# Moving the mixers' stores to GpSimd, with new mask arithmetic, selection groups and planner costs, in a one-core transformer layer

## The chip, the cores and the metric

The kernel runs on one core of one Trainium2 chip. The metric is the time of one execution on the device in microseconds (us), as the median of several runs. The engines are named as in the profile: PE is TensorE (PEld its weight loads), DVE is VectorE, ACT is ScalarE, POOL is GpSimd, SP is SyncE. ACTq and POOLq mark what the sequencer of an engine does beside its arithmetic, such as issuing a DMA from ACT.

## The reference

One decoder layer over 1024 tokens of width 1024: a half-step SwiGLU, two token mixers side by side, and a second half-step SwiGLU.

```python
x = x + 0.5 * swiglu(rms_norm(x), w1_gate, w1_up, w1_down)
c_q, k_a, v_a, k_idx, w_idx, q_b, k_b, v_b, gate_a, gate_b = split(rms_norm(x) @ w_in)
...
score = sum_h relu(q_idx[h] @ k_idx.T) * w_idx[h]      # indexer, 8 heads of 64
idx = top_k(where(causal, score, -inf), 256)           # 256 keys per query
y_a = softmax(q_a @ k_a[idx].T) @ v_a[idx] @ w_uv      # 8 heads, shared keys and values
...
z = q_b @ k_b.T / 8                                    # stick-breaking, 8 heads of 64
a = exp(log_sigmoid(z) + reverse_cumsum(log_sigmoid(-z)) - log_sigmoid(-z))   # strictly causal
y_b = a @ v_b
...
x = x + (sigmoid(gate_a) * (y_a @ w_oA) + sigmoid(gate_b) * (y_b @ w_oB)) @ w_out
x = x + 0.5 * swiglu(rms_norm(x), w2_gate, w2_up, w2_down)
```

## The kernel before

**Stages.** A SwiGLU stands at each end (0 to about 707 us, and from about 1530 us to the end). Between them lie the mixers: projections of keys, queries and index queries, the indexer's scores, the choice of 256 keys per query, stick-breaking attention, sparse attention, and the output projections. The 1024 queries are cut into 8 blocks of 128; block `i` sees `i + 1` blocks of keys, so its tiles are `128 x (i+1)*128`. Float32 operands are kept as a high and a low part, so that most results leave PSUM twice: ACT copies the high part, DVE subtracts it and keeps the low part. Both are stored to DRAM where a later stage loads them.

**The order.** In the mixers a build-time planner, `Weave`, writes the instruction order of PE, DVE, ACT and POOL. Each piece of work is a generator that yields the engine it wants next and the tiles it waits for; `Weave.cost` gives each instruction a duration, and `Weave.flush` adds up when engines and tiles come free; the ready piece that could start first is written next. The order is then fixed: each engine works through its own list, and an instruction whose input is late holds up everything behind it on that engine. The two SwiGLUs are not planned by `Weave`.

**Names.** `fillers` computes the projections of values, queries, keys and gates (`psf`, weights `wqk...`, `wg...`); `qk_out` evicts queries and keys into `evh` and `evl`, `gate_out` evicts gates into `evg`. These tiles, and `yh`, share one ring of three buffers, `evr`; a buffer is free again when its store has landed. `y_out` evicts a half of a head of stick-breaking attention: `yl` (a ring of one buffer) takes the sum, `yh` its high part, and then `yl` the low part; they are stored to `ybhd` and `ybld`, loaded later as `ybh` and `ybl`. `ka_out` and `key_out` evict values and keys of the sparse mixer.

`topk` finds the threshold of each query bit by bit: 31 rounds, each with one Sign activation on ACT for each block of the group (`junka`), then two small DVE operations. The six blocks with more than 256 keys are split into two groups; each group is one such stream. When the bits are known, one mask for each block is made (lines 1173 to 1186) and stored to `bd`, from where `hidden_keys` loads it as `bias`. Masks of the second group wait for the mark `top0`, and a bias tile for `top0` or `top1` of its group. Sparse attention takes the blocks in the order 1, 0, 5, 4, 7, 6, 3, 2; blocks 1 and 0 need no selection.

In the sticks, PE makes `psz`; ACT takes two sigmoids of it (`left`, `sa`); DVE scans and multiplies; PE transposes (`pstT`), ACT and DVE evict the two parts (`pt`), and PE multiplies by the values (`psy`). In sparse attention PE makes `psL`, DVE adds the bias and takes the maximum (`e`, `mx`, line 1732), ACT exponentiates (line 1744, after a table load at line 1742), DVE normalises (line 1747), PE transposes (`pspT`), and `pt` goes into `pso`. `psob` and `psoa` are output projections.

```python
put_high, put_low = nc.scalar.dma_start, nc.gpsimd.dma_start
```

## Time and profile before

| | us |
|---|---|
| median of 3 runs (2303.51 to 2309.24) | 2306.31 |
| the profiled execution's own time | 2300.48 |
| its span from the first instruction to the last | 2298.7 |

| engine | busy us | share of the span |
|---|---|---|
| PE | 2188.0 | 95% |
| DVE | 1590.1 | 69% |
| ACT | 1111.9 | 48% |
| POOL | 883.6 | 38% |

The shares are means over stages with different limits. For one stage the busy time of each engine in that stretch is compared with the stretch's length; where no engine fills it, the waits say which engine held up which. The profile gives the granted clock of TensorE as a share of full speed (2.4 GHz); 0.5 is its lower level, 1.2 GHz.

### The profile page before, as it was taken

The page shows a single profiled execution, that of the slowest core. Times are in us where ns is not written, and L with a number is a line of the kernel's source. Part 1 is how long each engine was busy: PE and PEld are TensorE (multiplying, and loading weights), DVE is VectorE, ACT ScalarE, POOL GpSimd, SP SyncE. Part 2 cuts the span into 40 slices and gives each one's busy share as a digit, 9 for nine tenths or more (in the row PEclk, how much of TensorE's full clock was granted, in tenths as well). Part 3 has the DMA queues.
Part 4 walks back from the last instruction along what each step waited for, and adds up shares of the span by engine and source line. Part 5 has one row for each costly group of instructions (what it writes and reads, how often), then busy time and mean ns, then how long its engine had stood idle before and what let it go on. Part 6 is the DMA issues. An engine that isn't in the chain of part 4 may idle for free.

```text
span 2298.7 us, 30186 instructions
## 1 busy us (share of the span) xinstructions
PE 2188.0 (95%) x10460; PEld 1808.7 (79%) x10460; DVE 1590.1 (69%) x2512; ACT 1111.9 (48%) x2133; POOL 883.6 (38%) x648
## 2 busy tenths in 40 slices
PE   7999999999999898889999699999999999999999
PEld 6788888888889777667788578877878888888877
DVE  5765656678862897667698877862476565667675
ACT  4323232344452479989988456633342323233443
POOL 3555555432262444211122133146345555543233
PEclk9999999999999999999999799999999999999999
DMA  5233333587663243645464533357323333358755
GB/s 166 75 117 97 114 95 114 167 310 239 165 215 113 81 133 101 172 97 120 112 142 115 173 112 96 127 182 253 118 65 106 101 108 99 110 167 288 244 161 183
DMA packets 252537, 330.64 MB, mean 144 GB/s; under 512 B 20576, under 2 KB 155376, under 8 KB 252384
## 3 DMA queue, kind: packets, MB, share of 16 engines
q1 hardware_dynamic: 235264, 288.83, 42.1%
q0 software_dynamic: 7488, 24.16, 2.8%
q10 hardware_dynamic: 9632, 15.73, 2.0%
q8 instruction: 82, 1.34, 0.2%
q14 instruction: 71, 0.58, 0.1%
HBM read 234.78 MB, written 93.88 MB: 143 GB/s over the span
## 4 chain that ended last, share of the span: by engine, by line
PE 67%; DVE 12%; ACT 10%; DMA 5%; issue 5%; POOL 1%; ACTq 1%; SPq 0%; DVEq 0%; POOLq 0%
PE p L676 5%; PE p L677 5%; PE p L675 4%; ACT junka L1130 4%; PE pc L466 3%; PE pc L467 3%; PE pc L468 3%; PE pd L468 3%; PE pd L466 3%; PE pd L467 3%; PE pa L468 3%; PE pa L466 3%; PE pa L467 3%; PE pb L468 2%; PE pb L467 2%
## 5 line engine op out<-in xcount | busy, mean ns | idle before, releaser
L1130 ACT ACTIVATE junka<-u,cand,sig 128x1024 bf16<-128x1024 f32 (+5 forms) x186 | 182.7, 982 | 22.6 <-DVE cand L1127 10.9
L1566 DVE TENSOR_TENSOR_SCAN left<-left 128x640 f32<-128x640 f32 (+3 forms) x64 | 92.8, 1450 | 3.8 <-ACT left L1558 3.8
L1615 DVE TENSOR_TENSOR pt<-pstT,pt 128x512 fp32r<-128x512 f32 (+1 forms) x96 | 51.2, 551 | 21.0 <-ACT pt L1613 20.4
L1732 DVE CUSTOM_DVE_ANT_0 e<-psL,bias 128x512 f32<-128x512 f32 (+3 forms) x96 | 49.4, 550 | 14.4 <-PE psL L1769 14.4
L1615 DVE TENSOR_TENSOR pt<-pspT,pt 128x512 fp32r<-128x512 f32 x72 | 46.6, 684 | 18.0 <-ACT pt L1613 18.0
L1744 ACT ACTIVATE e<-e,nm 128x256 f32<-128x256 f32 (+7 forms) x64 | 49.4, 774 | 18.5 <-DVE nm L1739 17.3
L1667 PE MATMUL pstT<-ident,sa 128*128 128x128 f32 x288 | 46.7, 276 | 12.1 <-DVE pt L1615 10.3
L1823 PE MATMUL pspT<-ident,e 128*128 128x128 f32 x288 | 42.1, 286 | 16.0 <-DVE ri L1746 9.0
L1569 DVE TENSOR_TENSOR sa<-sa,left 128x639 f32<-128x639 f32 (+3 forms) x64 | 53.1, 829 | 5.0 <-ACT sa L1560 1.8
L676 PE MATMUL p<-bT,bS 128*128 128x512 f32 x132 | 51.9, 393 | 2.9 <-DVE bT L377 2.9
L1634 POOL DMA_DIRECT2D ybld<-yl x16 | 8.8, 551 | 118.6 <-DVE yl L1632 79.7
L1667 PEld LDWEIGHTS pstT<-ident,sa 128*128 128x128 f32 x288 | 34.4, 140 | 25.1 <-DVE pt L1615 16.8
L1613 ACT ACTIVATE pt<-pspT 128x512 fp32r<-128x512 f32 x72 | 39.5, 596 | 29.6 <-PE pspT L1823 29.3
L1823 PEld LDWEIGHTS pspT<-ident,e 128*128 128x128 f32 x288 | 35.3, 146 | 22.4 <-DVE e L1747 9.5
L676 PE MATMUL p<-aT,aS 128*128 128x512 f32 x132 | 51.6, 391 | 1.0 <-DVE aT L377 1.0
L1479 DVE SCALAR_TENSOR_TENSOR u<-relu,WI,u 128x512 f32<-128x512 f32 (+1 forms) x70 | 49.6, 727 | 4.2 <-ACT relu L1472 3.0
L677 PE MATMUL p<-bT,bS 128*128 128x512 f32 x132 | 51.5, 393 | 1.0 <-POOL bS L377 1.0
L1613 ACT ACTIVATE pt<-pstT 128x512 fp32r<-128x512 f32 (+1 forms) x96 | 46.6, 501 | 9.8 <-PE pstT L1667 7.7
L677 PE MATMUL p<-aT,aS 128*128 128x512 f32 x132 | 50.5, 390 | 0.0
L1560 ACT ACTIVATE sa<-psz 128x512 f32<-128x512 f32 (+2 forms) x96 | 47.0, 503 | 5.0 <-ACT evg L1063 2.4
L1558 ACT ACTIVATE left<-psz 128x512 f32<-128x512 f32 (+2 forms) x96 | 45.3, 496 | 7.8 <-DVE cand L1161 1.6
L1472 ACT ACTIVATE relu<-psdot 128x512 f32<-128x512 f32 (+1 forms) x80 | 39.9, 520 | 16.6 <-DVE u L1479 9.9
(3061 smaller groups left out, 8296.4 us busy)
## 6 DMA issues: line engine op xcount, KB each, us to landing
aw<-in_w_down_dram SPq DMA_DIRECT2D x33, 512.0 KB, 4.8
bw<-in_w_down_dram SPq DMA_DIRECT2D x33, 512.0 KB, 4.5
a0r<-in_w_gate_dram SPq DMA_DIRECT2D x22, 512.0 KB, 4.3
a1r<-in_w_up_dram SPq DMA_DIRECT2D x22, 512.0 KB, 4.9
b0r<-in_w_gate_dram SPq DMA_DIRECT2D x22, 512.0 KB, 4.1
b1r<-in_w_up_dram SPq DMA_DIRECT2D x22, 512.0 KB, 4.8
x<-in_x_dram SPq DMA_DIRECT2D x16, 512.0 KB, 6.3
gd<-evg ACTq DMA_DIRECT2D x32, 256.0 KB, 2.8
```

What stands on the lines that cost most here:

```text
L466: nc.tensor.matmul(ps, a[:, c], b[k][:, HI], start=start and k == 0, stop=False, skip_group_check=True)
L467: nc.tensor.matmul(ps, a[:, c], b[k][:, LO], start=False, stop=False, skip_group_check=True)
L468: nc.tensor.matmul(ps, a[:, l], b[k][:, HI], start=False, stop=k == 3, skip_group_check=True)
L675: nc.tensor.matmul(ps[q][m], S[:, h], T[:, HI], start=p == 0, stop=False)
L676: nc.tensor.matmul(ps[q][m], S[:, h], T[:, LO], start=False, stop=False)
L677: nc.tensor.matmul(ps[q][m], S[:, l], T[:, HI], start=False, stop=p == last)
L1130: nc.scalar.activation(junks[1][:, 0:(i + 1) * P], score[i], AF.Sign, scale=sig[:, b:b + 1], bias=cand.bitcast(F32)[:, b:b + 1], accum_out ...
L1566: nc.vector.tensor_tensor_scan(back, back, back, 1.0, op0=ALU.mult, op1=ALU.bypass)
L1613: nc.scalar.activation(pt[:, off:512], tp[:, off:512], AF.Copy)
L1615: nc.vector.tensor_sub(pt[:, 512 + off:1024], tp[:, off:512], f32(pt[:, off:512]))
L1667: nc.tensor.transpose(tp[:, q * P:(q + 1) * P], A[n + q][:, j * P:(j + 1) * P], ident)
L1823: nc.tensor.transpose(tp[:, q * P:(q + 1) * P], E[n + q][:, j * P:(j + 1) * P], ident)
```

## The change

**Stores.** 74 stores that ACT issued (queries and keys, gates, the high parts of `va`, `ka` and `yh`) are issued by POOL (`put_low`), each as a step of its own that the planner places. **Costs.** The planner's ACT instructions with an accumulator cost 0.09 more and are ready 0.05 sooner, a store on ACT would cost 0.37 where it cost 0.05, and some DVE forms cost 0.06 or 0.11 more. **Groups.** The groups of the selection are blocks (5, 4, 2) and (6, 7, 3), which were (7, 2, 3) and (4, 5, 6). **Masks.** A mask is made from one Sign activation on ACT with the threshold as bias and the count as its accumulator, one comparison of its 16-bit result, the scan, a subtraction and one comparison. Before, there were two comparisons with the float32 scores, the scan, a comparison with a product, a sum and a scaling, all on DVE.

```diff
@@ Weave.cost and Weave.flush @@
-            return 0.055 + n / 1190 + 0.22 * (len(outs) > 1), 0.1 + 0.15 * (len(outs) > 1)
+            return 0.055 + n / 1190 + 0.31 * (len(outs) > 1), 0.1 + 0.1 * (len(outs) > 1)
...
-    groups = ((7, 2, 3), (4, 5, 6))
+    groups = ((5, 4, 2), (6, 7, 3))
@@ qk_out @@
             nc.scalar.activation(th, ps, AF.Copy, scale=sc)
-            put_high(qkd[nh_][pr * P:(pr + 1) * P, cols], f32(th))
             yield DVE, ps, th
             nc.vector.scalar_tensor_tensor(tl_, ps, sc, f32(th), op0=ALU.mult, op1=ALU.subtract)
-            give(ps, th)
+            give(ps)
+            yield POOL, th
+            put_low(qkd[nh_][pr * P:(pr + 1) * P, cols], f32(th))
+            give(th)
@@ gate_out @@
             nc.scalar.activation(ev, ps, AF.Sigmoid)
-            put_high(gd[g * P:(g + 1) * P, cols], ev)
-            give(ps, ev)
+            give(ps)
+            yield POOL, ev
+            put_low(gd[g * P:(g + 1) * P, cols], ev)
+            give(ev)
@@ topk @@
-            nc.vector.tensor_mul(Tf, Tf, sig)
+            nc.vector.scalar_tensor_tensor(fix, Tf, -1.0, sig, op0=ALU.mult, op1=ALU.mult)
...
-                yield DVE, (x2, 3)
+                yield ACT, (x2, 3), fix
...
-                nc.vector.tensor_scalar(eq, score[i], Tf[:, c], None, op0=ALU.is_equal)
-                yield DVE
-                nc.vector.tensor_scalar(gt, score[i], Tf[:, c], 0.0, op0=ALU.is_gt, op1=ALU.add, accum_out=cnt[:, c])
-                nc.vector.tensor_scalar(rem[:, c], cnt[:, c], -1.0, float(TOPK), op0=ALU.mult, op1=ALU.add)
+                nc.scalar.activation(gt, score[i], AF.Sign, bias=fix[:, c], accum_out=cnt[:, c])
+                yield DVE, gt
+                nc.vector.tensor_scalar(eq, gt, 0.0, STEP, op0=ALU.is_equal, op1=ALU.mult)
+                nc.vector.tensor_scalar(rem[:, c], cnt[:, c], -0.5 * STEP, (TOPK - 0.5 * nk) * STEP, op0=ALU.mult, op1=ALU.add)
                 yield DVE
                 nc.vector.tensor_tensor_scan(cum, eq, eq, 0.0, op0=ALU.add, op1=ALU.bypass)
                 yield DVE
-                nc.vector.scalar_tensor_tensor(eq, cum, rem[:, c], eq, op0=ALU.is_le, op1=ALU.mult)
-                yield DVE
-                nc.vector.tensor_add(gt, gt, eq)
+                nc.vector.scalar_tensor_tensor(rem[:, c], cum[:, nk - 1:nk], 0.5, rem[:, c], op0=ALU.mult, op1=ALU.add)
+                nc.vector.tensor_sub(eq, cum, gt)
...
-                nc.vector.tensor_scalar(bias, gt, -NEG, NEG, op0=ALU.mult, op1=ALU.add)
+                nc.vector.tensor_scalar(bias, eq, rem[:, c], NEG, op0=ALU.is_gt, op1=ALU.mult)
```

The stores in `ka_out`, `key_out` and `y_out` are moved in the same way; that of `yh` now stands on POOL ahead of that of `yl`. Line numbers of the changed kernel are a few higher than before.

What the planner makes of it differs in many places. On POOL, among the gates' weight splits (`wg10l` and so on, a subtraction of two 128x1024 tiles), there stood before:

```order
L974 TENSOR_TENSOR wg10l<-wg10r,wg10h 128x1024
L974 TENSOR_TENSOR wg11l<-wg11r,wg11h 128x1024
L1634 DMA ybld<-yl 64x512
L974 TENSOR_TENSOR wg12l<-wg12r,wg12h 128x1024
L1634 DMA ybld<-yl 64x512
L974 TENSOR_TENSOR wg13l<-wg13r,wg13h 128x1024
```

and now:

```order
L976 TENSOR_TENSOR wg10l<-wg10r,wg10h 128x1024
L1642 DMA ybhd<-yh 64x512
L1070 DMA gd<-evg 128x512
L1647 DMA ybld<-yl 64x512
L1642 DMA ybhd<-yh 64x512
L1070 DMA gd<-evg 128x512
L1647 DMA ybld<-yl 64x512
L976 TENSOR_TENSOR wg11l<-wg11r,wg11h 128x1024
L1070 DMA gd<-evg 128x512 x2
L976 TENSOR_TENSOR wg12l<-wg12r,wg12h 128x1024
```

So stores of gates and of `yh` stand between the splits, and pairs of gate stores behind a split.

On ACT, where the sticks end and the first exponentials (`e`) begin, there stood before:

```order
L1063 ACTIVATE evg<-psf 128x512
L1064 DMA gd<-evg 128x512
L1613 ACTIVATE pt<-pstT 128x256
L1628 ACTIVATE yh<-yl 64x512
L1630 DMA ybhd<-yh 64x512
L1613 ACTIVATE pt<-pstT 128x128
L972 ACTIVATE ob2h<-ob2r 128x1024
L1622 ACTIVATE yl<-psy 64x512
L1063 ACTIVATE evg<-psf 128x512
L1064 DMA gd<-evg 128x512
L1742 ACT_TABLE_LOAD
L1744 ACTIVATE e,ssum<-e,nm 128x256 x2
```

and now:

```order
L1633 ACTIVATE yl<-psy 64x512
L1624 ACTIVATE pt<-pstT 128x384
L1624 ACTIVATE pt<-pstT 128x256
L1639 ACTIVATE yh<-yl 64x512
L1624 ACTIVATE pt<-pstT 128x128
L1755 ACT_TABLE_LOAD
L1757 ACTIVATE e,ssum<-e,nm 128x256 x3
L1633 ACTIVATE yl<-psy 64x512
L1757 ACTIVATE e,ssum<-e,nm 128x256
L1639 ACTIVATE yh<-yl 64x512
L1181 ACTIVATE gt,cnt_6038<-u_7226,fix_11658 128x896
L1757 ACTIVATE e,ssum<-e,nm 128x256 x2
```

The table load moved from behind the last `yl` and the last gate to ahead of that `yl`, directly behind the last `pt` of the sticks, and the masks' Sign (`gt`) of block 6 stands among the exponentials.

On PE, at the same place, the last products `psy` of the sticks stood behind projections of gate 7, of which these are the last:

```order
L307 MATMUL psf<-mhi_5243,wg7h 128x512
L308 MATMUL psf<-mlo_5251,wg7h 128x512
L309 MATMUL psf<-mhi_5243,wg7l 128x512
L307 MATMUL psf<-mhi_5244,wg7h 128x512
L308 MATMUL psf<-mlo_5252,wg7h 128x512
L309 MATMUL psf<-mhi_5244,wg7l 128x512
L1647 MATMUL psy<-pt,vv 128x128
L1649 MATMUL psy<-pt,vv 128x128
L1823 MATMUL pspT<-ident,e 128x128 x8
```

and now there stands, with no projection of a gate left:

```order
L1680 MATMUL pstT<-ident,sa 128x128 x2
L1660 MATMUL psy<-pt,vv 128x512
L1662 MATMUL psy<-pt,vv 128x512
L1660 MATMUL psy<-pt,vv 128x384
L1662 MATMUL psy<-pt,vv 128x384
L1680 MATMUL pstT<-ident,sa 128x128
L1660 MATMUL psy<-pt,vv 128x256
L1662 MATMUL psy<-pt,vv 128x256
L1660 MATMUL psy<-pt,vv 128x128
L1662 MATMUL psy<-pt,vv 128x128
L1836 MATMUL pspT<-ident,e 128x128 x8
```

The gates' projections moved ahead, into the sticks. The order inside the two SwiGLUs is the same on every engine.

## Rows read from the trace of the kernel before

**Rows 1.** The page's first part: busy us, share of the span, instructions.

```profile
PE 2188.0 (95%) x10460; PEld 1808.7 (79%) x10460; DVE 1590.1 (69%) x2512; ACT 1111.9 (48%) x2133; POOL 883.6 (38%) x648
```

**Rows 2.** Stretches of the mixers: length, busy us by engine, clock, DMA share, GB/s.

```profile
707.00:840.00 133.00, 122.16 (x724) 106.33 (x725) 88.48 (x150) 56.93 (x116) 49.87 (x49) 0.96 0.38 106
840.00:1160.00 320.00, 285.31 (x1453) 228.00 (x1452) 229.01 (x431) 290.19 (x608) 75.52 (x67) 0.97 0.49 121
1160.00:1283.00 123.00, 122.52 (x634) 100.48 (x632) 110.14 (x211) 95.36 (x201) 27.07 (x17) 1.00 0.50 140
1283.00:1318.00 35.00, 16.79 (x64) 11.58 (x64) 28.46 (x93) 16.56 (x46) 4.00 (x4) 0.70 0.49 163
1318.00:1530.00 212.00, 202.17 (x1043) 167.75 (x1043) 158.56 (x425) 110.96 (x220) 60.69 (x54) 0.98 0.39 125
```

**Rows 3.** Waits of PE, 840 to 1160 us: total us, times, longest.

```profile
PE pstT L1667 <- DVE pt L1615: 10.3, 10, 2.2
PE psz L1589 <- ACT sa L1560: 10.1, 6, 2.3
PE psqt L1445 <- DVE qx L1441: 4.8, 1, 4.8
```

**Rows 4.** ACT's evictions with stores, 840 to 1160 us: count, busy us, mean ns, idle before.

```profile
L1063 ACT ACTIVATE evg<-psf 128x512 f32<-128x512 f32 x17 | 10.4, 614 | 1.1 <-PE psz L1593 0.6 <-ACT yh L1628 0.5
L1051 ACT ACTIVATE evh<-psf 128x512 fp32r<-128x512 f32 x11 | 6.6, 600 | 0.0
L1628 ACT ACTIVATE yh<-yl 64x512 fp32r<-64x512 f32 x8 | 5.0, 620 | 0.5 <-DVE pt L1615 0.5
```

**Rows 5.** ACT in order of time around one store: start us, length us.

```profile
935.50 0.33 ACTq L1052 DMA_DIRECT2D khd<-evh  x1
935.88 0.81 ACT L1130 ACTIVATE junka<-u,cand,sig 128x512 bf16<-128x512 f32 x1 [0.41 <-ACT evh L1051]
```

**Rows 6.** POOL's stores of `evl`: issue in ns, landing; then landing of ACT's `gd`.

```profile
L1057 POOL DMA_DIRECT2D kld<-evl x8: 539/575/631, 814.7 to 987.3; - x8
DMA to landing us min/median/max: 2.3/6.3/10.6
...
DMA to landing us min/median/max: 2.0/2.8/10.3
```

**Rows 7.** All engines in order of time at the sticks' end: start us, length us.

```profile
1279.09 0.54 POOL L1634 DMA_DIRECT2D ybld<-yl  x1 [9.70 <-DVE yl L1632]
...
1282.73 0.28 PE L1649 MATMUL psy<-pt,vv 128*128 128x128 f32 x1
...
1284.84 0.59 ACT L1622 ACTIVATE yl<-psy 64x512 f32<-64x512 f32 x1 [1.08 <-DMA ybld<-yl]
...
1286.44 1.28 ACT L1742 ACT_TABLE_LOAD   x1 [0.39 <-ACT evg L1063]
...
1290.38 0.49 ACT L1744 ACTIVATE e<-e,nm 128x256 f32<-128x256 f32 x1
...
1292.05 1.30 PE L1823 MATMUL pspT<-ident,e 128*128 128x128 f32 x3 [9.05 <-DVE ri L1746]
```

**Rows 8.** The masks' lines on DVE, 1283 to 1318 us: count, busy us, mean ns.

```profile
L1178 DVE TENSOR_TENSOR_SCAN cum<-eq 128x640 f16<-128x640 f16 (+2 forms) x3 | 5.2, 1748 | 0.0
L1175 DVE TENSOR_SCALAR_CACHE_REDUCE gt<-u,T 128x640 f16<-128x640 f32 (+2 forms) x3 | 3.0, 1000 | 0.0
L1180 DVE SCALAR_TENSOR_TENSOR eq<-cum,rem,eq 128x640 f16<-128x640 f16 (+1 forms) x2 | 1.9, 944 | 0.0
L1173 DVE TENSOR_SCALAR eq<-u,T 128x768 f16<-128x768 f32 (+1 forms) x2 | 1.3, 646 | 0.0
L1182 DVE TENSOR_TENSOR gt<-gt,eq 128x640 f16<-128x640 f16 (+1 forms) x2 | 1.0, 520 | 0.0
L1186 DVE TENSOR_SCALAR cum<-gt 128x640 bf16<-128x640 f16 (+1 forms) x2 | 0.7, 335 | 0.0
```

**Rows 9.** ACT's Sign on 896 keys, 707 to 1320 us: count, busy us, mean ns.

```profile
L1130 ACT ACTIVATE junka<-u,cand,sig 128x896 bf16<-128x896 f32 x31 | 35.6, 1148 | 2.4 <-ACT evg L1063 1.6 <-ACT yh L1628 0.5
```

More of the change, by code (lines that the diff above doesn't have):

```diff
@@ L129, in cost @@
             return 0.17 + n * (0.5 if any(a.dtype in (F32, F32R, I32) for a in wide) else 0.25) / 960, 0.08
-        return 0.07 + n / 960, 0.08
+        slow = getattr(i, "is_scalar_tensor_tensor", False) or len(ins) == 1 and len(outs[0].shape) == 2 and n > outs[0].free_size()
+        return 0.07 + 0.06 * slow + 0.11 * (outs[0].shape[0] < P) + n / 960, 0.08
     def hop(self, name, eng):
@@ L151, in flush @@
                 else:
-                    t = max(t, self.free[eng]) + (0.55 if eng == POOL else 0.05)
+                    t = max(t, self.free[eng]) + (0.55 if eng == POOL else 0.37)
                     self.free[eng], t, eng = t, t + 2.4 + mb / 0.25, "DMA"
@@ L906, in trunk @@
         ctx1.close()
+    STEP = 2.0 ** -12
     WI = cst.tile([P, NT, H], F32, name="WI")
-    groups = ((7, 2, 3), (4, 5, 6))
+    groups = ((5, 4, 2), (6, 7, 3))
     order = groups[0] + groups[1]
@@ L1179, in topk @@
                 yield DVE
-                nc.vector.scalar_tensor_tensor(eq, cum, rem[:, c], eq, op0=ALU.is_le, op1=ALU.mult)
-                yield DVE
-                nc.vector.tensor_add(gt, gt, eq)
-                give(tiles[0], tiles[2])
+                nc.vector.scalar_tensor_tensor(rem[:, c], cum[:, nk - 1:nk], 0.5, rem[:, c], op0=ALU.mult, op1=ALU.add)
+                nc.vector.tensor_sub(eq, cum, gt)
+                give(tiles[2])
                 bias = tiles[1].bitcast(BF16)[:, 0:nk]
                 yield DVE
-                nc.vector.tensor_scalar(bias, gt, -NEG, NEG, op0=ALU.mult, op1=ALU.add)
+                nc.vector.tensor_scalar(bias, eq, rem[:, c], NEG, op0=ALU.is_gt, op1=ALU.mult)
+                give(tiles[0])
                 yield POOL, tiles[1]
@@ L1306, in ka_out @@
             nc.scalar.activation(va[:, 0:P], ps[:, 64:192], AF.Copy)
-            put_high(vad[0][:, m], f32(va[:, 0:P]))
+            yield POOL, va
+            put_low(vad[0][:, m], f32(va[:, 0:P]))
             yield DVE, bank, va
@@ L1319, in key_out @@
             nc.scalar.activation(h_, ps, AF.Copy)
-            put_high(kad[0][:, cols], f32(h_))
+            yield POOL, ka
+            put_low(kad[0][:, cols], f32(h_))
             yield DVE, ps, ka
@@ L1629, in y_out @@
             cols = slice(c * 512, c * 512 + 512)
-            put_high(ybd[0][h * HD:(h + 1) * HD, cols], f32(yh[0:HD]))
+            yield POOL, yh
+            put_low(ybd[0][h * HD:(h + 1) * HD, cols], f32(yh[0:HD]))
             yield DVE, yl, yh
             nc.vector.tensor_tensor(yl[0:HD], yt, f32(yh[0:HD]), op=ALU.subtract)
+            give(yh)
             yield POOL, yl
             put_low(ybd[1][h * HD:(h + 1) * HD, cols], yt)
-            give(yl, yh)
+            give(yl)
         def value_products(h, c, pts, outs):
```

## The prediction

> **What bounds the kernel now.** I read the page's first part first: PE is busy 95% of the span [rows 1], so all that any change of order can give back is PE's idle time, and time in which PE runs at its lower clock. The change touches the mixers alone, so the next view is the table of stretches [rows 2], cut where the character of the work changes. In its rows compare PE's busy time with the length. From 707 to 840 us 10.8 us are missing, from 840 to 1160 us 34.7, from 1160 to 1283 us 0.5, from 1283 to 1318 us 18.2, and from 1318 to 1530 us 9.8. So there are two places to look at: the long stretch in which sticks, selection rounds and projections run together, and the short one in which the sticks end and sparse attention begins.
>
> In the long stretch ACT is busy 290.2 of 320 us [rows 2]. The page doesn't count a store that ACT issues as busy time, but it occupies the engine: behind an `evh` the store goes out at 935.50, and the next activation starts at 935.88, 0.41 us after the eviction ended [rows 5]. ACT evicts 17 gates, 11 query or key tiles and 8 `yh` there [rows 4], and each has a store: 36 x 0.41 = 14.8 us. With them ACT is occupied 305 of 320 us, 95%. The waits of PE agree that ACT is the limit: it waited 10.1 us for `sa` and 10.3 us for `pt` from DVE, which itself follows ACT's `pt` [rows 3]; 20.4 us in all. The stretch from 1160 to 1283 us is PE's own: nothing done to ACT or DVE can shorten it.
>
> At the sticks' end the rows in order of time tell the story [rows 7]. The last product of the sticks ends at 1283.0. The first exponential needs the table load, which starts at 1286.44, because ACT first runs the last `yl` and the last gate; that `yl` waited until 1284.84 for its one buffer, whose store POOL had issued at 1279.09, 5.75 us before. PE starts its first `pspT` at 1292.05, after 9.05 us idle. The granted clock is 0.70 over the stretch [rows 2]: part of it ran at 1.2 GHz after that idleness. DVE is busy 28.5 of the 35 us, and 13.1 of those are the masks of the second group [rows 8], because blocks 5 and 4 come right behind blocks 1 and 0 and belong to that group.
>
> **The change part by part.** *Stores off ACT.* Of the 74 stores, 36 lie in the long stretch and are worth 14.8 us of an engine occupied 95% of it. Not all of it comes back: the wait for `qx`, 4.8 us [rows 3], doesn't hang on ACT. Bounds: nothing, if PE then waits for DVE's half of each eviction instead; 20.4 us, if both waits go, helped by a planner that now knows how long ACT takes and puts projections where PE used to wait. I take 13, near the stores' own price, because the price is a sum of rows and the help by the planner is not. The stores before 840 us lie on an ACT that is busy 57 of 133 us, and those from 1160 to 1283 us beside a full PE [rows 2]: nothing.
>
> *Stores onto POOL.* Each takes 0.55 us to issue, at most 0.63 in this line [rows 6]; 36 x 0.55 = 20 us on a POOL that is busy 75.5 of 320 us [rows 2]. That is hidden by POOL's own idle time. What it delays is the landing, and so the ring of three buffers. Landing took 2.3 to 10.6 us from POOL and 2.0 to 10.3 from ACT [rows 6], so it is much the same; the new part is the queue on POOL, a split or a store ahead. Cover: 36 evictions and 11 further `evl` in 320 us are one buffer each 6.8 us, so three buffers stand 20 us of holding; a hold of 11 us with 3 us of queue fits. I take nothing; the bound above is among the rivals.
>
> On the same POOL stores the Trainium skill speaks against this change (SBUF — State Buffer, section SBUF: two separate sides): a DMA issued from GpSimd has its descriptors written by that engine, and DVE in a two-port mode locks it out meanwhile, so that the store waits although no wire is busy. The trace doesn't show it, since no issue of this line took over 0.63 us with DVE busy 229 of 320 us [rows 2, 6]. By the page's measured pair, 0.62 us alone and 3.1 us beside a DVE copy, 36 stores would hold POOL for 112 us, an estimate from that page; POOL has 244 us free, so the sum stays the same.
>
> *Groups and masks at the sticks' end.* Blocks 5 and 4 are now in the first group, whose masks are made during the sticks, so bias tiles are there when `psL` of block 5 comes. The masks of blocks 6 and 7 still fall among the exponentials of blocks 1 and 0, but are cheaper on DVE: scans 1.748 x 1920 / 768 = 4.4 us (1920 keys for both, 768 the mean of the three sizes in the row), subtractions 0.520 x 1920 / 704 = 1.4, four 16-bit operations 0.335 x 1920 / 704 / 2 = 0.46 on average, 1.8, and small ones 0.6: 8.2 us where there were 13.1 [rows 8]. In exchange ACT gets two Signs, about 1.15 and 1.3 us [rows 9] and 0.2 each to read the accumulator. DVE is the busier of the two there, so I take 4.9 less half of the 2.9, about 3.5.
>
> *The table load.* It moves ahead of the last `yl`, directly behind the last `pt`, so three exponentials run at once. The fourth still stands behind `yl`, which needs the store of the `yl` before. From the end of `yh` that takes some 0.8 for DVE's low part (an estimate from ACT's 0.62 for the same tile [rows 4] and the steps between engines), 5.75 from the issue to `yl`, and 0.59 [rows 7]: 7.2 us. The end of `yh` is now some 1.2 us ahead of the last product (the last `pt`, its low part and the product, each of 128 columns and near the 0.28 of that product), so the fourth exponential starts 6.0 us behind it, where it was 7.4 (1290.38 less 1283.0). That is 1.4 us; with a landing of 2.3 us it would be 4. I take 2. With less idleness, less of the stretch runs at the lower clock: PE's 16.8 us at 0.70 are 5 us lost; I take 2 of these back. Together 3.5 + 2 + 2 = 7.5 us. Bounds: a loss of 3, if the two Signs delay each group of exponentials in full and the landing takes 10 us; 18 if all idle time goes.
>
> *The drain.* Before, projections of gate 7 stood between the last products; now none does. The last half head has four steps of transposing, ACT's `pt`, DVE's `pt` and a product. A round is at least an eviction by ACT, 0.6 us for 512 columns [rows 4], and as much again on DVE, and some of these rounds are bare. I charge 3 us, between nothing and 6.
>
> *The rest.* The index stage (10.8 us idle) keeps its order but for stores; the sparse part (9.8 us idle) runs the same work with the projections spread anew. I take nothing, give or take 3 us.
>
> Sum: -13 - 7.5 + 3 = -17.5 us against the profiled execution: a span of 2298.7 becomes 2281, its own time 2300.5 becomes 2283. That execution stands 5.8 us below the median of 2306.3, so the median becomes 2289.
>
> **The rivals.** *All of it comes back.* If the new order fits the engines well, the long stretch gives 20.4 us, the lower clock in it (0.97 of 285 us is 8.6 us) goes as well, and the sticks' end gives 10: together 39 us less 3 for the drain, or 2270. For it: the waits are short and many, which is what an order made with wrong durations gives. Against it: PE's order is fixed, so each wait must go by itself. *Nothing comes back.* ACT's freed 14.8 us turn into waits for DVE, whose `pt` already ends 10.3 us of PE's waits, and the drain eats the sticks' end: -5 to 0, or 2303. For it: DVE is busy 229 of 320 us and holds scans of 1.4 us. *POOL holds the ring.* A store waits on POOL behind a step that isn't ready, its buffer is not free, ACT's next eviction stands still, and with it all of ACT. It decides where a buffer is held over 20 us, three times the 6.8 us above, or where three are taken within a few us. If each of the 32 gate evictions waited 0.8 us, that is 26 us on ACT against 14.8 saved, 11 us slower, or 2317. Against it: in that stretch no wait of the 17 gate evictions was put down to a landing, with landings up to 10.3 us in the run [rows 4, 6]. The rule of the Trainium skill (SBUF — State Buffer, section SBUF: two separate sides) would act at this place and in this sense.
>
> **How the numbers follow.** Chances: my forecast (10 to 28 us less) 0.53, all comes back 0.14, nothing comes back 0.20, the ring 0.13. A measurement of this kernel tells about 0.3%, 6.9 us, from no change. The forecast and the first rival are faster than that, and a little of the second; the third is slower: faster 0.67, same 0.20, slower 0.13. The range goes from 2264, somewhat beyond the first rival, to 2311, where it leaves out most of the third. The forecast's own range is 2278 to 2297.
>
> **What would show it.** No store on ACT's queue; in the stretch of about 840 to 1150 us PE's waits for `sa` and `pt` under half of 20.4 us; the sticks' end with the table load within 1 us of the last product and masks of about 8 us; a drain of bare `pt` rounds of about 3 us. Wrong would be: waits of ACT's `evg` or `evh` for landings of over 5 us in sum, POOL issues well over 0.63 us, or PE's missing time in the long stretch still near 35 us with DVE named.

## The result, and the profile after

The changed kernel takes 2275.53 us (median of 4 runs, 2274.65 to 2278.45), the kernel before 2306.49 us in the runs beside it. The ratio is 0.9868, with a 95% interval of 0.9851 to 0.9885: 30 us faster, 26 to 34. Between the two profiled executions it is 2300.48 less 2276.41, 24.1 us. That is in the forecast's sense and inside the predicted range, 13.5 us better than the forecast of 2289.

The first part of the page, to be held against [rows 1]: PE's busy time is about the same, and POOL has 74 instructions more.

```profile
PE 2183.0 (96%) x10460; PEld 1811.1 (80%) x10460; DVE 1576.1 (69%) x2500; ACT 1110.5 (49%) x2145; POOL 925.9 (41%) x722
```

The stretches of the mixers, with columns as in [rows 2], cut at the last product of the sticks (1275.5) and at the first `psob` (1315.2):

```profile
840.00:1160.00 320.00, 296.77 (x1506) 239.32 (x1505) 232.57 (x424) 292.25 (x620) 106.27 (x110) 0.97 0.50 126
1160.00:1275.50 115.50, 110.96 (x572) 90.83 (x570) 100.01 (x199) 99.54 (x209) 33.66 (x35) 0.99 0.51 155
1275.50:1315.20 39.70, 26.61 (x87) 19.14 (x87) 36.09 (x136) 20.70 (x57) 2.99 (x6) 0.64 0.30 88
1315.20:1508.00 192.80, 190.89 (x1024) 161.49 (x1023) 148.45 (x395) 106.85 (x213) 61.09 (x53) 0.99 0.43 137
```

PE's missing time in the long stretch went from 34.7 to 23.2 us. Behind the sticks it was 18.2 + 9.8 = 28.0 us in the last two rows of [rows 2], and is now 13.1 + 1.9 = 15.0. The last product of the sticks ends 7.5 us sooner (1275.5 for 1283.0), the first `psm` starts 22.4 us sooner (1499.1 for 1521.5), and the SwiGLU behind it gives the rest. So what lies ahead of the last product gave a third, and what lies behind it two thirds.

PE's waits from 840 to 1160 us, against [rows 3]:

```profile
PE psf L308 <- DVE evl L1055: 8.1, 2, 7.8
PE pstT L1680 <- DVE sa L1580: 5.6, 4, 2.4
PE psz L1600 <- ACT sa L1571: 3.9, 2, 3.5
...
PE pstT L1680 <- DVE pt L1626: 1.4, 3, 0.6
```

The waits for ACT's `sa` and DVE's `pt` fell from 20.4 to 5.3 us, as said; that for DVE's part of `sa`, which the prediction didn't count, rose from 1.5 to 5.6. New is a wait of 7.8 us, and its cause is the ring of three buffers. In order of time on POOL, DVE and PE:

```profile
941.34 0.60 POOL L1058 DMA_DIRECT2D qhd<-evh  x1 [3.07 <-ACT evh L1053]
...
955.88 0.69 DVE L1055 SCALAR_TENSOR_TENSOR evl<-psf,evh 128x512 fp32r<-128x512 f32 x1 [10.12 <-DMA qhd<-evh]
...
956.63 0.80 PE L308 MATMUL psf<-mhi,wqk10323h 128*128 128x512 f32 x1 [7.76 <-DVE evl L1055]
```

DVE can't write `evl` until the `evh` of the projection before has landed, 14.4 us after its issue at 941.34, and PE's next projection has no bank until `evl` is out.

The sticks' end in order of time, against [rows 7]:

```profile
1274.39 1.28 ACT L1755 ACT_TABLE_LOAD   x1
...
1275.21 0.33 PE L1662 MATMUL psy<-pt,vv 128*128 128x128 f32 x1 [0.35 <-DVE pt L1626]
...
1277.54 0.59 ACT L1633 ACTIVATE yl<-psy 64x512 f32<-64x512 f32 x1 [0.27 <-DMA ybld<-yl]
...
1278.43 0.51 ACT L1757 ACTIVATE e<-e,nm 128x256 f32<-128x256 f32 x1 [0.29 <-DVE nm L1752]
...
1279.59 0.96 PE L1836 MATMUL pspT<-ident,e 128*128 128x128 f32 x2 [4.05 <-DVE nm L1752]
```

The table load starts 1.15 us ahead of the end of the last product, the fourth exponential 2.9 us behind it, and PE is idle 4.05 us there where it was 9.05. Ahead of it PE waits once more: its row at 1268.93 has 3.89 us for DVE's `pt`. In that time DVE ended the selection of the second group, and one of its small operations ran as long as a subtraction on POOL:

```profile
1264.26 2.35 POOL L976 TENSOR_TENSOR ob2l<-ob2r,ob2h 128x1024 fp32r<-128x1024 f32 x1 [9.36 <-ACT ob2h L974]
1264.28 2.35 DVE L1142 TENSOR_SCALAR T<-T 128x3 int32<-128x3 int32 x1
...
1268.93 0.66 PE L1680 MATMUL pstT<-ident,sa 128*128 128x128 f32 x4 [3.89 <-DVE pt L1626]
```

### The profile page after: what moved, and what is told of

Read it like the earlier page. It is cut to its first block, busy times and chain, and to the rows that moved or that the text cites. A ratio compares the mean times of both kernels' runs of the same rounds, so it can differ in the third digit from the quotient of the medians.

```text
span 2274.6 us, 30225 instructions
## 1 busy us (share of the span) xinstructions
PE 2183.0 (96%) x10460; PEld 1811.1 (80%) x10460; DVE 1576.1 (69%) x2500; ACT 1110.5 (49%) x2145; POOL 925.9 (41%) x722
## 4 chain that ended last, share of the span: by engine, by line
PE 70%; DVE 10%; DMA 7%; ACT 6%; issue 5%; POOL 2%; SPq 0%; ACTq 0%; DVEq 0%; POOLq 0%
PE p L677 5%; PE p L678 5%; PE p L676 5%; PE pc L467 3%; PE pc L469 3%; PE pc L468 3%; PE pd L469 3%; PE pd L467 3%; PE pd L468 3%; PE pa L469 3%; PE pa L467 3%; PE pa L468 3%; ACT junka L1136 2%; PE pb L467 2%; PE pb L469 2%
## 5 line engine op out<-in xcount | busy, mean ns | idle before, releaser
L1136 ACT ACTIVATE junka<-u,cand,sig 128x768 bf16<-128x768 f32 (+4 forms) x186 | 183.3, 985 | 10.8 <-DVE cand L1133 9.0
L1577 DVE TENSOR_TENSOR_SCAN left<-left 128x640 f32<-128x640 f32 (+3 forms) x64 | 88.1, 1378 | 3.4 <-ACT left L1569 3.3
L1580 DVE TENSOR_TENSOR sa<-sa,left 128x639 f32<-128x639 f32 (+3 forms) x64 | 58.6, 918 | 3.7 <-ACT sa L1571 0.4
L1680 PE MATMUL pstT<-ident,sa 128*128 128x128 f32 x288 | 47.0, 278 | 11.1 <-DVE sa L1580 5.6
L1624 ACT ACTIVATE pt<-pspT 128x512 fp32r<-128x512 f32 x72 | 39.7, 596 | 36.2 <-PE pspT L1836 35.9
L1757 ACT ACTIVATE e<-e,nm 128x256 f32<-128x256 f32 (+7 forms) x64 | 49.4, 774 | 13.0 <-DVE nm L1752 11.3
L1680 PEld LDWEIGHTS pstT<-ident,sa 128*128 128x128 f32 x288 | 34.7, 141 | 22.4 <-DVE pt L1626 9.0
L1624 ACT ACTIVATE pt<-pstT 128x512 fp32r<-128x512 f32 (+1 forms) x96 | 46.3, 505 | 11.2 <-PE pstT L1680 10.1
L1899 POOL TENSOR_TENSOR o<-o,gate 128x512 f32<-128x512 f32 x16 | 21.8, 1360 | 65.2 <-ACT o L1894 65.2
```

Source lines behind the costliest of these rows:

```text
L1136: nc.scalar.activation(junks[1][:, 0:(i + 1) * P], score[i], AF.Sign, scale=sig[:, b:b + 1], bias=cand.bitcast(F32)[:, b:b + 1], accum_out ...
L1577: nc.vector.tensor_tensor_scan(back, back, back, 1.0, op0=ALU.mult, op1=ALU.bypass)
L1624: nc.scalar.activation(pt[:, off:512], tp[:, off:512], AF.Copy)
L1680: nc.tensor.transpose(tp[:, q * P:(q + 1) * P], A[n + q][:, j * P:(j + 1) * P], ident)
```

## The experiments

Each run is compared with the kernel before on the same chip; gains in us are its ratio's distance from 1, times 2304.

**One part at a time on the kernel before.** The edits are the four parts of the diff above, each alone.

```diff
@@ stores only: here gate_out; the same in qk_out, ka_out, key_out and y_out @@
-            put_high(gd[g * P:(g + 1) * P, cols], ev)
...
+            yield POOL, ev
+            put_low(gd[g * P:(g + 1) * P, cols], ev)
...
@@ groups only @@
-    groups = ((7, 2, 3), (4, 5, 6))
+    groups = ((5, 4, 2), (6, 7, 3))
@@ masks only: topk as in the change, of which one line @@
+                nc.scalar.activation(gt, score[i], AF.Sign, bias=fix[:, c], accum_out=cnt[:, c])
@@ costs only: Weave.cost and Weave.flush as in the change, of which one line @@
-                    t = max(t, self.free[eng]) + (0.55 if eng == POOL else 0.05)
+                    t = max(t, self.free[eng]) + (0.55 if eng == POOL else 0.37)
```

> The kernel before with only the stores moved: 74 stores issued by GpSimd as steps of their own; planner costs, groups and masks as before. Stores theory: this alone gives about 11 to 15 us, since 36 stores of 0.41 us leave ScalarE in the long stretch; the waits of PE for sa and pt there, 20.4 us before, fall under 10 us, and the sticks' end and the sparse part change by less than 4 us. Costs theory (the stores help only with a planner that knows ScalarE's real durations): under 5 us. Ring theory: waits for landings eat it, 0 or some us slower.

> The kernel before with only the groups (5, 4, 2) and (6, 7, 3). Stores theory: 3 to 6 us faster, all of it behind the sticks, where the masks of blocks 5 and 4 no longer fall among the first exponentials; idle time of PE from the last product of the sticks to the first psm, 27.7 us before, falls by 3 to 6. Groups theory: the fall of 12.9 us in that idle time which the changed kernel shows is all due to the groups, so 10 to 15 us faster. Costs theory: no change, within 3 us.

> The kernel before with only the new masks (one Sign on ScalarE, a 16-bit comparison). Stores theory: 2 to 5 us faster, since the masks between 1283 and 1318 us take DVE some 8 instead of 13 us. Groups theory: 0 to 2 us. Masks theory: 6 us or more faster, DVE being what the sparse part waits for. Against all of them: the Signs delay the exponentials, and it is 1 to 3 us slower.

> The kernel before with only the planner's three cost lines (a store on ScalarE 0.37 instead of 0.05, accumulators 0.31 and 0.1, slower forms of DVE); all stores are still ScalarE's. Stores theory: within 5 us of the kernel before, since ScalarE keeps its 14.8 us of stores in the long stretch. Costs theory: 10 to 20 us faster, with PE's waits for sa and pt between 840 and 1160 us falling from 20.4 to under 10 us without any store moved.

Stores 2287.29 us, 0.9934 (0.9917 to 0.9951); groups 2291.59, 0.9949 (0.9934 to 0.9965); masks 2296.91, 0.9974 (0.9962 to 0.9986); costs 2290.49, 0.9940 (0.9925 to 0.9955). Each alone is a gain, 15.2, 11.8, 6.0 and 13.8 us. They add up to 47, and together they give 30, so they overlap. The times of stores, groups and costs are about those of the theories named after them; that of the masks lies at the bound between two.

The stores' gain is as large as the prediction's first term, but it isn't found where the term put it. PE's missing time from 840 to 1160 us is 35.5 us, where it was 34.7: the waits for `sa` and `pt` fell to 10.1 us, and one wait of 11.9 us, put down to a round of the selection, came in their place.

```profile
840.00:1160.00 320.00, 284.46 (x1461) 230.84 (x1460) 231.83 (x440) 285.82 (x613) 101.86 (x107) 0.96 0.49 123
```

```profile
PE pstT L1675 <- ACT junka L1134: 11.9, 1, 11.9
```

The groups' gain lies behind the first `psob`: from there to the first `psm` PE's missing time is 3.8 us, where it was 9.8.

```profile
1320.40:1509.50 189.10, 185.27 (x1007) 156.89 (x1005) 151.69 (x419) 109.11 (x222) 54.22 (x49) 1.00 0.41 131
```

The run that told most is the last, costs alone. Its long stretch, and PE's waits there (of the two that are in question, both rows stand here):

```profile
840.00:1160.00 320.00, 308.03 (x1592) 251.12 (x1591) 240.62 (x427) 283.75 (x604) 85.26 (x71) 0.98 0.51 130
```

```profile
PE psz L1590 <- ACT sa L1561: 3.1, 3, 2.4
...
PE pstT L1668 <- DVE pt L1616: 0.9, 3, 0.5
```

No store has moved, 41 are ACT's in this stretch, and the waits are 4.0 us; PE works 308.0 of 320 us. ACT is about as full as before: 283.8 us busy and 19.0 idle at the 41 stores make 303 us, against 290.2 and 16.0 at 36 stores, 306. So these waits didn't need a much freer ACT: another order removes them too. What it won there it lost behind the sticks. The rows are PE's waits from 1266 to 1345 us:

```profile
PE psL L1769 <- DVE mx L1733: 12.7, 3, 11.2
PE pspT L1824 <- DVE e L1748: 9.2, 6, 3.0
PE psya L308 <- ACT o L1882: 8.1, 1, 8.1
```

**The queue alone, in an unchanged order.** The planner is told an engine for each store that differs from the engine that issues it, so that the order of all arithmetic stays word for word the same.

```diff
+            eng = self.plan.get(n, str(i.engine).split(".")[-1])
@@ kernel before, its order, the 74 stores on GpSimd @@
+    put_high, put_low = put_as(nc.gpsimd.dma_start, ACT), nc.gpsimd.dma_start
@@ changed kernel, its order, the 74 stores on ScalarE @@
+    put_back, put_low = put_as(nc.scalar.dma_start, POOL), nc.gpsimd.dma_start
```

> The kernel before in its own order, in which only the queue of the 74 stores changes: the planner still counts them as ScalarE's, so TensorE, VectorE and the arithmetic of ScalarE and GpSimd keep their order. Occupancy theory (each store takes 0.41 us of a ScalarE that is the limit in the long stretch): 10 to 15 us faster, PE's waits for sa and pt between 840 and 1150 us fall from 20.0 to under 10 us. Order theory (PE waits there because its list was written with wrong durations, and ScalarE has time enough): within 4 us of before, those waits stay above 14 us, and the gain of the run with only the stores moved was the new order. Ring theory: slower, with waits of ScalarE for landings.

> The changed kernel in its own order, in which only the queue of the 74 stores goes back to ScalarE: the planner still counts them as GpSimd's, and all arithmetic keeps its order. Occupancy theory: 8 to 15 us slower than the changed kernel (2284 to 2291 us), with PE's waits for sa and pt in the long stretch back above 15 us. Order theory: within 4 us of the changed kernel's 2275.5; less idle time at 956 us, where a landing held PE for 7.8 us, may even make it 3 faster.

The order of before with stores on POOL: 2296.92 us, 0.9972 (0.9959 to 0.9985), 6.5 us faster (3.5 to 9.4), between the two theories. Its waits:

```profile
PE psz L1599 <- ACT sa L1570: 5.7, 5, 2.3
PE pstT L1677 <- DVE pt L1625: 5.6, 5, 2.6
...
PE psf L308 <- ACT evg L1073: 4.3, 2, 3.0
```

The two waits fell from 20.4 to 11.3 us, and a new one for `evg` took 4.3 of that. So the 6.5 us are net of that wait, in an order that was not made for stores on POOL.

The order of after with stores on ACT: 2273.77 us, 0.9880 (0.9860 to 0.9900), not to be told from the changed kernel's 0.9868. Its long stretch:

```profile
840.00:1160.00 320.00, 300.83 (x1527) 242.81 (x1526) 234.17 (x430) 297.26 (x629) 84.18 (x72) 0.98 0.51 128
```

ACT is busy 297.3 us and issues 41 stores, and PE still does 300.8 us of work, more than in the changed kernel. But these stores don't cost ACT 0.41 us each. To be held against [rows 5]:

```profile
937.07 0.57 ACT L1063 ACTIVATE evh<-psf 128x512 fp32r<-128x512 f32 x1
937.55 0.80 ACT L1146 ACTIVATE junka<-u,cand,sig 128x512 bf16<-128x512 f32 x1
937.67 0.33 ACTq L730 DMA_DIRECT2D qhd<-evh  x1
```

In the old order a store stands directly behind the eviction that fills its tile, and ACT stands still for it. Here another activation stands between them, and the store goes out while that one runs. Added up over the stretch, ACT is idle 16.0 us at the 36 stores of the kernel before, and 0.6 us at these 41. The stall at the ring is there too, 5.0 us where it was 7.8, so it is the order's more than the queue's.

So the occupancy theory, which is the prediction's first term, holds for the old order at half its size. In the new order there is nothing for it to give, since stores placed like this take almost no time of ACT on either queue. Whether the new order would suffer from an ACT that lost 17 us is not tested by this run.

**The changed kernel without one part.** Stores back to ACT with the planner told so; the old groups; the old costs.

```diff
@@ all but stores: here gate_out @@
-            yield POOL, ev
-            put_low(gd[g * P:(g + 1) * P, cols], ev)
...
+            put_high(gd[g * P:(g + 1) * P, cols], ev)
...
@@ all but groups @@
-    groups = ((5, 4, 2), (6, 7, 3))
+    groups = ((7, 2, 3), (4, 5, 6))
@@ all but costs: one line of three @@
-                    t = max(t, self.free[eng]) + (0.55 if eng == POOL else 0.37)
+                    t = max(t, self.free[eng]) + (0.55 if eng == POOL else 0.05)
```

> The changed kernel without the moved stores: they are ScalarE's, planned at 0.37 us each; costs, groups and masks are new. Occupancy theory: 8 to 15 us slower than the changed kernel, 2284 to 2291 us. Order theory: within 5 us of the changed kernel, 2271 to 2281, since a planner that knows what a store costs has given the long stretch an order without those waits already in the run with only the costs changed.

> The changed kernel with the old groups (7, 2, 3) and (4, 5, 6). Occupancy theory with small gain from the groups: 3 to 6 us slower than the changed kernel, 2279 to 2282 us. Groups theory (the sparse part's fall in idle time is the groups', since with old groups the projections are used up before it and nothing covers its waits): 9 to 16 us slower, 2285 to 2292 us, with PE idle between the last product of the sticks and the first psm above 25 us, where the changed kernel has 14.8 and the run with only the costs changed had 39.

> The changed kernel with the planner's old costs: stores on GpSimd, new groups and masks. In its order the last round of the selection stands shortly before the first exponential, as in the changed kernel. Selection theory: within 6 us of the changed kernel, 2270 to 2282. Costs theory (the new durations are what makes the order fit): 8 us or more slower, 2284 to 2295.

Without the stores 2305.18 us, 1.0013 (0.9998 to 1.0028): nothing is left of the gain, which neither theory expected. Without the groups 2291.09, 0.9951 (0.9932 to 0.9969): they are worth 0.0083, 19 us, in the changed kernel, about what the groups theory said. PE's missing time from the first `psob` to the first `psm` is then 11.5 us, where it was 1.9:

```profile
1313.40:1520.40 207.00, 195.46 (x1007) 163.23 (x1005) 155.72 (x421) 109.34 (x219) 55.08 (x51) 0.95 0.38 126
```

Without the costs 2269.42, 0.9850 (0.9837 to 0.9864), the fastest of all, against the costs theory, and 4 us ahead of the changed kernel by the ratios, whose intervals overlap.

The first of these looks like a proof that the stores had to leave ACT, but the run with the changed order and ACT's stores has shown that they cost nothing there. What differs is the planned order: the stores stand behind their evictions again, and other work stands elsewhere. For the run without moved stores, two views of a tile follow (durations in ns, first and last start): the selection's rounds on ACT from 1200 us on, of which each ends with such a reading, and the masks' stores on POOL.

```profile
L1132 ACT ACTIVATION_READ_ACCUMULATOR junka<-u,cand,sig x37: 185/188/268, 1202.4 to 1306.9; 128x1 f32 x37
```

```profile
L1193 POOL DMA_DIRECT2D bd<-cum x6: 539/558/585, 1259.2 to 1341.0; - x6
```

The last reading starts at 1306.9 us, 32 us behind the last product of the sticks (1275.0), and its last mask leaves at 1341.0; in the changed kernel those are 1262.6 and 1313.7. Selection and masks then fall among the exponentials. The stretch from there to its first `psob`, where PE is busy 35.5 of 59.4 us:

```profile
1275.00:1334.40 59.40, 35.53 (x118) 25.33 (x119) 48.45 (x188) 38.68 (x90) 2.23 (x4) 0.66 0.18 56
```

**Moving the selection by one number.** From this came a new theory: the place of the selection's end sets the time. The planner breaks ties by a number that each round of the selection carries; a smaller one lets the round be taken sooner.

```diff
@@ all but stores, with 1.4; changed kernel, with 4.0; changed kernel, with 1.5 @@
-                        yield ACT, cand, score[i], 2.0
+                        yield ACT, cand, score[i], 1.4
```

> The changed kernel with the stores left on ScalarE (planned at 0.37 us), as in the run that gained nothing, and one number more: the tie value of the selection's rounds is 1.4 instead of 2.0, so that the planner takes them sooner. In its order the last round stands before the first exponential, where it stood behind it. Selection theory (the time is set by where the selection ends against the sticks, since the second group's masks are late otherwise, and the moved stores helped by letting the planner write the rounds sooner): the last round starts at least 8 us before the last product of the sticks, 2275 to 2285 us. Store theory (the stores must leave ScalarE's list for the rest to pay): within 8 us of the 2305 us of that run.

> The changed kernel with one number changed: the tie value of the selection's rounds is 4.0 instead of 2.0, so that they come later. In its order the last round stands behind the first exponentials. All stores are GpSimd's. Selection theory: the last round starts some 15 us or more behind the last product of the sticks, the second group's masks are stored later than 1315 us, and the time goes up by 12 to 30 us, 2288 to 2305. Store theory and costs theory: within 5 us of the changed kernel's 2275.5.

> The changed kernel with the tie value of the selection's rounds at 1.5 instead of 2.0, a little sooner. Selection theory: the selection no longer sets the start of the sparse part of the changed kernel, whose idle time from the first output projection to psm is 1.8 us, so sooner gives nothing more: within 5 us of 2275.5. If the time falls on with an earlier end of the selection: 2265 to 2270.

Sooner without the stores: 2289.30 us, 0.9935 (0.9921 to 0.9949). One tie number gave 18 us by the ratios, with every store on ACT and planned there; that is half of what was missing, and less than expected. Later in the changed kernel: 2296.84, 0.9966 (0.9955 to 0.9977), 23 us lost, as expected. Sooner in the changed kernel: 2287.12, 0.9930 (0.9916 to 0.9943), 14 us lost, against the expectation. So a late selection is costly, but an early one isn't free either. In that last run the long stretch has these waits of PE, the first of them again for the ring:

```profile
PE psf L308 <- DVE evl L1055: 11.8, 4, 4.6
PE psdot L1513 <- ACT relu L1483: 3.9, 6, 1.2
```

From 1250 to 1290 us, when its projections are used up (the last ends at 1254.6) and the sticks have nothing beside them:

```profile
PE pstT L1680 <- DVE sa L1580: 12.3, 3, 8.9
```

All runs side by side: the ratio of the medians, and times of the trace in us. These are the start of the last reading in the selection's rounds, the ends of the last projection (`psf`) and the last product of the sticks (`psy`), the last mask's store, and the first `psm`. A trace is one execution, and it lies up to 6.4 us from the median of its runs, so smaller differences between rows say little.

| run | ratio | last round | last psf | last psy | last mask | first psm |
|---|---|---|---|---|---|---|
| before | 1 | 1267.7 | 1282.8 | 1283.0 | 1322.1 | 1521.5 |
| stores only | 0.9934 | 1259.5 | 1279.4 | 1269.1 | 1311.7 | 1512.8 |
| groups only | 0.9949 | 1266.4 | 1290.2 | 1278.5 | 1319.3 | 1509.5 |
| masks only | 0.9974 | 1257.8 | 1285.7 | 1282.9 | 1312.9 | 1519.2 |
| costs only | 0.9940 | 1295.9 | 1240.7 | 1266.7 | 1321.3 | 1515.3 |
| before's order, POOL | 0.9972 | 1264.2 | 1279.3 | 1279.5 | 1318.3 | 1518.1 |
| after | 0.9868 | 1262.6 | 1263.0 | 1275.5 | 1313.7 | 1499.1 |
| after's order, ACT | 0.9880 | 1255.8 | 1256.2 | 1268.7 | 1306.1 | 1492.2 |
| all but stores | 1.0013 | 1306.9 | 1250.6 | 1275.0 | 1341.0 | 1530.9 |
| all but groups | 0.9951 | 1280.9 | 1255.7 | 1280.8 | 1319.3 | 1520.4 |
| all but stores, sooner | 0.9935 | 1273.3 | 1231.5 | 1290.0 | 1323.8 | 1512.5 |
| after, later | 0.9966 | 1281.5 | 1262.8 | 1246.4 | 1319.9 | 1513.6 |
| after, sooner | 0.9930 | 1255.5 | 1254.6 | 1288.5 | 1309.9 | 1509.6 |
| all but costs | 0.9850 | 1251.7 | 1266.7 | 1244.9 | 1287.5 | 1487.2 |

The fastest run has sticks and selection done early and projections left to run behind the sticks. Four of the slower ones miss one of the three: a late selection (all but stores; after, later), or projections used up long before the sticks end (all but stores, sooner: 58 us before; after, sooner: 34). The three don't account for every run: "stores only" and "groups only" end the selection ahead of the sticks and have projections left, and are 0.0066 and 0.0081 above the changed kernel, whose own projections end 12.5 us ahead of its sticks.

## Why the prediction came out right, and where its steps did not

The sense and the range held. The result lies 2.5 us below the forecast's own range of 2278 to 2297 and 5.5 above the rival "all of it comes back" (2270), but not by that rival's mechanism, since the long stretch gave 11.5 us of idle time and not 20.4 and more. The division among the steps held only in part, and that the sum came out inside the range is in part luck: the sparse part, which was put at nothing, gave 7.9 us, and the sticks' end, which was put at 7.5, gave little.

**Stores off ACT, -13.** The sign that was named came true: `sa` and `pt` from 20.4 to 5.3 us, and the stretch's missing time fell by 11.5. The cause given was that ACT is the limit, and that was mis-sized: with the order held fixed, moving the queue gave 6.5 us (3.5 to 9.4) in the old order, and nothing that can be told in the new one, where the stores cost ACT 0.6 us in all. The stores alone, planned as POOL's, left the stretch's missing time at 35.5 us. The same waits vanish with every store on ACT when only the costs change. The step that failed is "the waits of PE agree that ACT is the limit": an engine that is occupied 95% and is waited for often may be short of time, or served in the wrong sequence, and the trace of one order doesn't tell these apart. The price of 0.41 us is right for a store directly behind its eviction, and is no fixed price of a store. Most of what the stores gave, they gave by being planned as steps of POOL: with all of them on ACT's queue, the kernel takes 0.9880 when they are planned so and 1.0013 when they are planned as ACT's, and in the second the selection ends 44 us later than in the changed kernel.

**Stores onto POOL, 0.** The issues stayed short. The views of three tiles of the changed kernel: the gates' stores, the query stores (issue in ns), and the landing of all that leaves an `evh`, in us:

```profile
L1070 POOL DMA_DIRECT2D gd<-evg x32: 542/568/588, 975.0 to 1266.6; - x32
```

```profile
L1058 POOL DMA_DIRECT2D qhd<-evh x8: 542/579/615, 778.3 to 948.9; - x8
```

```profile
DMA to landing us min/median/max: 2.7/6.1/14.4
```

The rule of the Trainium skill (SBUF — State Buffer, section SBUF: two separate sides), by which DVE in a two-port mode would hold up descriptors written on GpSimd, isn't seen: no issue in these rows took more than 0.615 us, with DVE busy 232.6 of 320 us. No row tells in which mode DVE's operations ran, so this doesn't test the rule. The ring rival did come true once, 7.8 us at 956 us, through `evl`, which takes a second buffer for each projection of queries or keys. The prediction counted holds on average, one buffer each 6.8 us, and a hold of 11; here two projections, with two buffers each, came 6.9 us apart, and the landing took 14.4.

**Sticks' end, -7.5.** Table load, fourth exponential and masks moved as described; PE's idle time there fell from 18.2 to 13.1 us, 5.1. The masks on DVE, between 1275.5 and 1318 us, are now three, of 2432 keys:

```profile
L1187 DVE TENSOR_TENSOR_SCAN cum<-eq 128x896 f16<-128x896 f16 (+2 forms) x3 | 5.5, 1838 | 0.0
...
L1190 DVE TENSOR_TENSOR eq<-cum,gt 128x896 f16<-128x896 f16 (+2 forms) x3 | 1.7, 576 | 0.0
L1194 DVE TENSOR_SCALAR cum<-eq,rem 128x896 bf16<-128x896 f16 (+2 forms) x3 | 1.3, 424 | 0.0
L1184 DVE TENSOR_SCALAR eq<-gt 128x896 f16<-128x896 f16 (+2 forms) x3 | 1.1, 365 | 0.0
```

That is 9.6 us, or 7.6 for the 1920 keys of the estimate, which was 7.6 without its small operations. The estimate left out block 3, the third of the second group. DVE is busy 36.1 of the 39.7 us there, a larger share than before. The fourth exponential came 2.9 us behind the last product and not 6.0: from the end of `yh` (1273.55) to that of the next `yl` (1278.13) it took 4.6 us, where the prediction had 7.2. The clock gave nothing back, where the prediction took 2 us: it was 0.64 in this stretch, 0.70 before [rows 2]. By the prediction's own reckoning 26.6 us of work at 0.64 lose 9.6 us, where 16.8 us at 0.70 lost 5.0. So of the 5.1 us less idle time some 4.6 went to the clock, an estimate from these rows.

**The drain, +3.** The size is near, since PE's missing time from 1160 us to the last product went from 0.5 to 4.5 us, but the mechanism is another. There was no chain of bare rounds: the two waits in the last rounds are 0.29 and 0.35 us, and the 3.89 us ahead of them are DVE's. From 1263.90 to 1268.46 us it ran the end of the selection, which is one step to the planner, before it came to `pt`; one operation on 128x3 took 2.35 us beside POOL's subtraction, and those around it 0.15 to 0.21. That POOL held it up is read from the times, and no run has moved the subtraction.

**The rest, 0 ± 3.** This is the other term that was mis-sized: the sparse part behind the first `psob` lost 7.9 us of idle time, 9.8 to 1.9. The prediction priced the groups at the sticks' end alone, within 3.5 us for groups and masks. They are worth 11.8 us alone (8 to 15) and 19 in the changed kernel, and the place is shown in both directions: this part's idle time goes from 9.8 to 3.8 us with the groups alone, and from 1.9 to 11.5 without them. "Groups only" and "all but groups" store the last mask at the same time, 1319.3 us, and their first `psm` stand 10.9 us apart. Why the groups carry so far is shown only in part: with the old groups blocks 4 and 5, wanted third and fourth, belong to the late masks, with the new ones blocks 6 and 7. The first `psm` stands 194 to 206 us behind the last mask's store in the six runs with the old groups, and 185 to 200 in the eight with the new ones; that goes together in fourteen runs, and is no proof of the cause.

**What stays open.** Each run with another plan has an order of its own, so a part's worth includes that order; only the two runs with a fixed order are free of it, and the second of them moved stores that cost ACT almost nothing. Where the gain of the stores alone lies is open: its profile books 2175.2 us of busy time on PE for the same products, 12.8 less than before, and hardly less idle time. That the projections' place matters beside the selection's is read from the table and the waits, and no run has moved the projections alone. The masks were tried alone only, not taken out of the changed kernel. Whether the fastest run really beats the changed kernel was not settled.

## What to carry to other kernels

Where a planner writes the order, test a change of resources with the order held fixed; otherwise the gain of the resource and that of the new order can't be told apart, and the second was here the larger. Look also at what the resource costs in that order: the same store took 0.41 us of ACT in one place and almost nothing in another. A wait for a busy engine doesn't show by itself that the engine is short of time, since the order and the durations may not fit: try the durations or a tie number before moving work. Milestones (the last round, the last filler, the last product, the last mask) told more here than busy shares, though not everything, and better durations made the last version no faster.

## What the runs showed of the hardware

A store that stood directly behind its eviction on ScalarE kept it idle 0.40 to 0.58 us (36 stores, 16.0 us, from 840 to 1160 us in the kernel before). A store with another activation in between went out beside that activation: 41 stores, 0.6 us in all, in the changed order with ACT's stores.

In the changed kernel's trace eight VectorE operations on 128x3 between 707 and 1530 us took over 0.6 us, up to 2.38, and each of them overlaps an operation of two inputs on GpSimd; the one shown above ends with it.

Landing of an `evh`, in us (least, median, most), in the pairs with one order: 2.0/2.2/11.1 when ACT issued the stores and 2.3/2.9/11.4 when POOL did, in the order of before; 2.0/4.5/11.9 and 2.7/6.1/14.4 in the order of after. So the order moved the median more than the queue did. The ring's stall was 5.0 us with ACT's stores and 7.8 with POOL's. All of these are one profile each.
